# Four small edits to a scatter-add kernel: a PSUM bank, a split one-hot, a later payload and a later flag product

## The chip, the core and the metric

The kernel runs on one core of one Trainium2 chip. Its engines are TensorE (PE in the profile, its weight loads PEld), VectorE (DVE), ScalarE (ACT), GpSimd (POOL) and SyncE (SP), each with a queue of its own that it works off in order. The metric is the device time of one execution in microseconds, the median of several runs.

## The reference

There are 4096 nodes with 128 float features each and 65536 edges, drawn at random. Every edge adds the feature row of its source node to the output row of its destination node.

```python
def reference(node_features, edge_index_src, edge_index_dst):
    output = np.zeros((num_nodes, dim), dtype=np.float32)
    for i in range(len(edge_index_src)):
        output[edge_index_dst[i]] += node_features[edge_index_src[i]]
    return output
```

## The kernel before, in words

The kernel never gathers a row. It sorts the edges by blocks of 128 nodes in two passes, and then does the whole sum as dense matmuls: for every block of destinations and every block of sources, a product of two one-hot matrices gives the 128x128 matrix of edge counts between them, and that matrix is multiplied by the features of the sources.

**First pass.** The edges are split into 24 chunks, taken as six quads (`NQ = 6`, so index 4 is the fifth quad). For each quad, `buckets1` makes one-hots of the destination block, `counts` makes ranks out of them with matmuls into four PSUM banks that carry the tag `psA` (ScalarE copies each out as `cum`), and `move1` moves the edges: for each of four parts `l`, VectorE makes one-hots `p` of the ranks (line 210, the helper `onehot`, three windows each) and TensorE multiplies them with the payloads into the bank `psm` (line 295). Behind the four parts ScalarE copies `psm` out as `sbk` and `sa` (lines 299 and 300). `psm` has the tag `misc`, which is a single bank. While the moves of quad `q` run, the function `beside` does the bucket work of group 0 for earlier quads: `buckets0` compares `sbk` (VectorE, line 380), TensorE makes column sums of that (`pst`, line 389), `scan0` scans these on VectorE (line 394), `counts0` and `ranks0` go on with them.

**Second pass and main loop.** Eight groups of four destination blocks follow (`GROUPS`), each with four slots of the main loop, 32 slots in all. In a slot, `blocks` makes the count matrices of 8 steps in two halves of four (line 688, sixteen matmuls a half, into `psA` banks, copied out as `a` by ScalarE, line 690), and `product` multiplies them by the features (line 695, eight matmuls a half, into `pso`). The one-hots `oh` of a slot are made one slot ahead by `onehots`: one VectorE instruction for the source keys (`slo`) and one for the destination keys (`dlo`), over 32 columns each; only for slot 0 these are split into two parts of 16 columns. Beside this, the groups to come are prepared by the steps of `pass2(g)`: which step runs in which slot is written out in `STEPS` (group g from 3 on in slots 4g-10, 4g-9, 4g-8, 4g-4 and 4g-3). The first step of a group makes `buckets` (VectorE, line 538) and then, on GpSimd, `two_chunks`, the sums of two chunks (line 554); the second is `before_all`, twelve matmuls on those sums into `psb` (line 564, in the `misc` bank) and a ScalarE copy (line 566); the third is `running_by_two` (lines 577 and 581), `masked` (line 586) and `payloads` (line 547), all on GpSimd; the fourth adds halves and makes ranks; the fifth moves the edges. A dictionary `owed` holds back the payloads of group 3: they run at the end of the first step of group 4.

After every fourth slot `evacuate` and `finish` bring the sums of four slots out: ScalarE copies `pso`, TensorE transposes it into `psx` (line 314, the `misc` bank), ScalarE copies that to `rows` (line 316), and SyncE writes it out. At the end of slot 28 (`slots - 4`) `flag` checks whether any bucket overflowed: VectorE reduces the ranks to a column `fall`, TensorE sums it over the partitions into `psf` (line 712, `misc` too), and VectorE writes a flag (line 713) that decides about a general path behind the kernel.

The order of the work on each engine is the order of the program; nothing is rearranged. A tile waits for the readers of the tile that had its buffer before.

Of the kernel before, what the change touches and what calls it, by code (L numbers as in the profile page):

```python
# [8 lines left out]
P = 128  # L9
F32 = mybir.dt.float32  # L10
# [11 lines left out]
NQ = NCH // 4  # L22
# [18 lines left out]
def kernel(  # L41
# [32 lines left out]
    with ExitStack() as fast:  # L74
        fast.enter_context(tc.manual_schedule())
        _fast(fast, tc, node_features, src32, dst32, out, ident, fmax, flag_i, T)
# [6 lines left out]
def _fast(ctx, tc, X, src32, dst32, out, ident, fmax, flag_i, T):  # L83
# [7 lines left out]
    ps = ctx.enter_context(tc.tile_pool(name="ps", bufs=2, space=bass.MemoryType.PSUM))  # L91
# [115 lines left out]
    def onehot(dst, keys2, n, m=P, io=None, m0=0):  # L207

        io = (piota if io is None else io)[:, None, m0:m0 + m].to_broadcast([P, n, m])
        V.tensor_tensor(  # L210
            out=dst.rearrange("p i (m k) -> p i m k", k=2),
            in0=io.rearrange("p i (m k) -> p i m k", k=2),
            in1=keys2[:, :, None, :].to_broadcast([P, n, m // 2, 2]), op=OP.is_equal)
# [63 lines left out]
    def place(q):  # L277

        at = (q % 2 * QH + q // 2) * 4
        return slice(at, at + 4)  # L280
# [2 lines left out]
    sbk = sb1.tile([P, NCH, NB], BF16, name="sbk")  # L283

    def move1(q, meanwhile):
        psm = ps.tile([P, 512], F32, name="psm", tag="misc", bufs=1)
        for l in range(4):
            t = p1[l // 2]
            n = len([j for j in range(NJ) if j * NCH + q * 4 + l < T])
            for j0, j1, m0, m1 in WIN:  # L290
                j1 = min(j1, n)
                onehot(t[:, l % 2, j0:j1, m0:m1], rank1[q][:, l, j0:j1], j1 - j0, m1 - m0, m0=m0)
            meanwhile(l)
            for j in range(n):
                PE.matmul(out=psm[:, l * 64:(l + 1) * 64], lhsT=t[:, l % 2, j, :],  # L295
                          rhs=v1[q][:, 4 * j + l].bitcast(BF16),
                          start=j == 0, stop=j == n - 1)
        pv = psm[:, :256].rearrange("p (l b k) -> p l b k", l=4, k=2)
        S.copy(out=sbk[:, place(q), :], in_=pv[:, :, :, 0])
        S.copy(out=sa[:, place(q), :], in_=pv[:, :, :, 1])  # L300
# [4 lines left out]
    def evacuate(k, pso):  # L305
        res = sb2.tile([P, 512], F32, name="res")
        S.copy(out=res[:], in_=pso[:])
        done.append((k, res))

    def finish():  # L310
        for k, res in done:
            psx = ps.tile([P, 512], F32, name="psx", tag="misc", bufs=1)
            for i in range(4):
                PE.transpose(psx[:, i * P:(i + 1) * P], res[:, i * P:(i + 1) * P], ident[:])
            rows = sb2.tile([P, 4, P], F32, name="rows", bufs=1)
            S.copy(out=rows[:].rearrange("p i f -> p (i f)"), in_=psx[:])
            nc.sync.dma_start(
                out=out[4 * k * P:4 * (k + 1) * P, :].rearrange("(i p) f -> p i f", p=P),
                in_=rows[:])
        done.clear()  # L320
# [180 lines left out]
    for q in range(NQ):  # L501
        if q == NQ - 1:
            p2c = sb1.tile([P, 2, NCH, P], BF16, name="p2c", tag="o2")
            p2b += [p2c[:, 0], p2c[:, 1]]
        move1(q, during(q))
        if q + 4 < NQ:
            buckets1(q + 4)
            column_sums1(q + 4)
        if q < 2:
            x_part(q + 2, 0)  # L510
        if q + 2 < NQ:
            spread1(q + 2)
# [6 lines left out]
    def pass2(g):  # L519
# [143 lines left out]
        both = tuple(each(*fs) for fs in zip(*[p[:2] for p in pairs])) + pairs[1][2:]  # L663
        ahead = owed.pop(g - 1, lambda: None)
        fs = [running_by_two, masked]
        if g == 3:
            owed[g] = payloads
        else:
            fs.append(payloads)
# [4 lines left out]
    def onehots(slot):  # L674

        oh = sb1.tile([P, 2, 4 * 8, P], BF16, name="oh", tag=f"t2{slot % 2}")
        at = slot % 4 * 32
        for i, n in ((0, 16), (16, 16)) if slot == 0 else ((0, 32),):
            if i:
                buckets_2()  # L680
            for k, io in ((0, piotas), (1, piota)):
                onehot(oh[:, k, i:i + n], keys2[slot // 4][k][:, at + i:at + i + n], n, io=io)
        return oh

    def blocks(k, oh, a):
        psa = ps.tile([P, 512], F32, name="psa", tag="psA", bufs=4)
        for i in range(4):
            PE.matmul(out=psa[:, i * P:(i + 1) * P], lhsT=oh[:, 0, 4 * k + i, :],  # L688
                      rhs=oh[:, 1, 4 * k + i, :], start=True, stop=True)
        S.copy(out=a[:, k, :], in_=psa[:])  # L690

    def product(k, slot, a, pso):
        s = slot % 4 * 8 + k
        for v in range(2):
            PE.matmul(out=pso[:], lhsT=xr[s // 16][:, s % 16, v, :], rhs=a[:, k, :],  # L695
                      start=s == 0 and v == 0, stop=s == NB - 1 and v == 1)

    def flag():

        ng = len(GROUPS)  # L700
        full = sb1.tile([P, NCH * NB], BF16, name="full", tag="o0")
        V.tensor_single_scalar(out=full[:], in_=sbk[:].rearrange("p c b -> p (c b)"), scalar=0.5,
                               op=OP.is_gt)
        V.tensor_reduce(out=fmax[:, ng:ng + 1], in_=full[:], op=OP.add, axis=AX.X)
        V.tensor_reduce(out=fmax[:, :ng], op=OP.max, axis=AX.X,
                        in_=rank2[:].rearrange("p g j c u k -> p g (j c u) k")[..., 0])
        V.tensor_scalar(out=fmax[:, :ng], in0=fmax[:, :ng], scalar1=63.5, scalar2=float(2 * P * T),
                        op0=OP.is_gt, op1=OP.mult)
        fall = sb1.tile([P, 1], F32, name="fall")
        V.tensor_reduce(out=fall[:], in_=fmax[:, :ng + 1], op=OP.add, axis=AX.X)  # L710
        psf = ps.tile([P, 512], F32, name="psf", tag="misc", bufs=1)
        PE.matmul(out=psf[:1, :1], lhsT=fall[:], rhs=one[:], start=True, stop=True)
        V.tensor_single_scalar(out=flag_i[:], in_=psf[:1, :1], scalar=float(P * T),
                               op=OP.not_equal)

    todo = [[]] + [pass2(g) for g in range(1, len(GROUPS))]

    def run(fs):
        for f in fs:
            f()  # L720
# [36 lines left out]
    sums_1()  # L757
    counts_1()
    oh = onehots(0)
    slots = NB  # L760
    prev, pso = None, None
    late = {}
    for slot in range(slots):
        for f in late.pop(slot, ()):
            f()
        steps = [todo[g].pop(0) for g in STEPS.get(slot, ())]
        late[slot + 2] = [f for st in steps for f in st[2:]]
        cur = oh
        if slot + 1 < slots:
            oh = onehots(slot + 1)  # L770
        if slot == 0:
            halves_1()
        if slot - 1 not in LATER and slot != 1:
            run(st[0] for st in steps)
        a = sb1.tile([P, 8, 4 * P], F32R, name="a", tag=f"A{slot % 2}")
        if slot % 4 == 0:
            pso = ps.tile([P, 512], F32, name="pso", tag="pso", bufs=1)
        for k in range(4):
            blocks(k, cur, a)
        if slot == 0:  # L780
            for k in range(4):
                product(k, slot, a, pso)
            before_all_2()
            running_2()
        if slot == 1:
            ranks_1()
            run(st[0] for st in steps)
        if slot > 1:
            for k in range(4, 8):
                product(k, *prev)  # L790
            if prev[0] % 4 == 3:
                evacuate(prev[0] // 4, prev[2])
        for k in range(4, 8):
            blocks(k, cur, a)
        if slot - 1 in LATER:
            run(later)
            run(st[0] for st in steps)
        if slot == 2:
            payloads_2()
        for k in range(4, 8) if slot == 0 else range(4):  # L800
            product(k, slot, a, pso)
        finish()
        later = [st[1] for st in steps if len(st) > 1]
        if slot not in LATER:
            run(later)
        prev = (slot, a, pso)
        if slot == slots - 4:
            flag()
    assert not any(todo[1:])
    for k in range(4, 8):  # L810
        product(k, *prev)
# [90 lines left out]
```

## Time and profile before

| | |
|---|---|
| median of three runs | 279.84 us (279.72 to 279.94) |
| the profiled execution | 280.0 us, of which 278.3 us lie in the span of its instructions |
| busy: TensorE, its weight loads | 264.6 us (95%), 223.2 us (80%) |
| busy: VectorE, ScalarE, GpSimd | 240.9 us (87%), 188.8 us (68%), 197.2 us (71%) |
| mean granted TensorE clock | 0.998 of full speed |

The span is what the profile covers, from the first instruction to the last. Busy shares are averages over stages with different limits; a matmul's end is modelled, so the busy time of TensorE is a little too long and its idle time a little too short.

### The profile page before, as it was taken

Reading aid. Unit: us, or ns where it says so; the run is one execution under the profiler, and the core shown is the slowest. Engines: PE = TensorE matmul, PEld = TensorE weight load, DVE = VectorE, ACT = ScalarE, POOL = GpSimd, SP = SyncE. Lnnn points to the kernel's source line nnn. Section 1 sums busy time; section 2 is a strip of 40 time slices with the busy share of each in tenths; the row PEclk is TensorE's granted clock in tenths of the full one; section 3 lists DMA queues with packets and bytes.
Section 4 is the critical chain, followed back from the end, with each engine's and each line's share of the span. In section 5 each row is a group of like instructions: output and inputs, shape, how many; then the busy total and the mean of one; then the engine's idle time right before and its main releaser. Section 6 shows DMA issues by size and latency. Waiting matters only on the chain.

```text
span 278.3 us, 8026 instructions
## 1 busy us (share of the span) xinstructions
PE 264.6 (95%) x3466; PEld 223.2 (80%) x3466; DVE 240.9 (87%) x239; ACT 188.8 (68%) x403; POOL 197.2 (71%) x205
## 2 busy tenths in 40 slices
PE   7599998998999999999989999999999999999994
PEld 6488887895888788888878888888888788877882
DVE  3989986999999989999997999899898899887801
ACT  1867777247676757777657687867776776877771
POOL 7499999848699989999998997999699400000000
PEclk9999999999999999999999999999999999999999
DMA  7800000000000010001000100100010001001001
GB/s 231 224 2 4 5 5 2 2 5 0 2 2 1 2 38 2 2 1 40 2 0 0 40 2 1 40 4 0 2 38 2 0 2 38 2 2 39 0 4 39
DMA packets 8725, 5.77 MB, mean 21 GB/s; under 512 B 240, under 2 KB 8432, under 8 KB 8688
## 3 DMA queue, kind: packets, MB, share of 16 engines
q1 hardware_dynamic: 8272, 4.59, 5.8%
q10 hardware_dynamic: 416, 0.66, 0.8%
q8 instruction: 27, 0.44, 0.7%
q14 instruction: 10, 0.08, 0.1%
HBM read 3.15 MB, written 2.10 MB: 19 GB/s over the span
## 4 chain that ended last, share of the span: by engine, by line
PE 63%; POOL 16%; DVE 11%; ACT 4%; issue 3%; DMA 2%; DVEq 0%; POOLq 0%
PE pso L695 29%; PE psa L688 14%; DVE oh L210 7%; PE psm L295 5%; POOL cum L586 5%; POOL v L547 4%; PE psr L257 3%; POOL cum L577 3%; ACT cum L252 3%; POOL two L554 2%; POOL cum L581 2%; PE ps L615 2%; DMA raw<-in_edge_index_dst_dram 2%; PE psc L249 2%; PE psc L245 2%
## 5 line engine op out<-in xcount | busy, mean ns | idle before, releaser
L690 ACT CAST a<-psa 128x512 fp32r<-128x512 f32 x256 | 131.7, 604 | 27.1 <-PE psa L688 27.0
L695 PE MATMUL pso<-a,xr 128*128 128x512 f32 x512 | 133.6, 403 | 0.1
L695 PEld LDWEIGHTS pso<-a,xr 128*128 128x128 f32 x512 | 91.1, 189 | 17.5 <-ACT a L690 1.6
L210 DVE TENSOR_TENSOR oh<-psi,slo 128x4096 bf16<-128x4096 uint16 (+1 forms) x33 | 73.2, 2219 | 9.1 <-PE psa L688 9.1
L210 DVE TENSOR_TENSOR oh<-psi,dlo 128x4096 bf16<-128x4096 uint16 (+1 forms) x33 | 73.1, 2216 | 0.0
L688 PE MATMUL psa<-oh 128*128 128x128 bf16 x1024 | 68.6, 220 | 1.0 <-ACT cum L648 0.6
L688 PEld LDWEIGHTS <-oh 128*128 128x128 bf16 x1024 | 57.9, 98 | 13.4 <-issue 12.2
L547 POOL TENSOR_TENSOR v<-oh,sa 128x512 bf16<-128x512 bf16 x42 | 42.6, 1056 | 1.9 <-DVE oh L538 1.9
L586 POOL TENSOR_TENSOR cum<-cum,oh 128x512 bf16<-128x512 bf16 x36 | 40.6, 1169 | 0.0
L273 POOL TENSOR_TENSOR v<-oh,kab 128x704 f32<-128x704 bf16 x24 | 32.9, 1406 | 5.5 <-ACT kab L185 4.4
L210 DVE TENSOR_TENSOR p<-psi,rank 128x448 bf16<-128x448 uint16 (+3 forms) x72 | 29.7, 479 | 0.0
L577 POOL TENSOR_TENSOR cum<-cum,two 128x256 bf16<-128x256 bf16 x25 | 19.2, 769 | 6.9 <-ACT cum L566 5.3
L252 ACT ACTIVATE cum<-psc,minus 128x512 bf16<-128x512 f32 (+1 forms) x36 | 21.0, 650 | 2.4 <-PE psc L249 1.7
L295 PE MATMUL psm<-v,p 128*128 128x64 bf16 x512 | 18.5, 193 | 1.6 <-ACT sa L300 1.4
L295 PEld LDWEIGHTS <-p 128*128 128x128 bf16 x512 | 16.8, 98 | 2.0 <-issue 1.3
L554 POOL TENSOR_TENSOR two<-oh 128x512 bf16<-128x512 bf16 x15 | 17.1, 1170 | 0.0
L581 POOL TENSOR_TENSOR cum<-cum,oh 128x512 bf16<-128x512 bf16 x15 | 17.0, 1163 | 0.0
L210 DVE TENSOR_TENSOR p2a<-psi,rank 128x3072 bf16<-128x3072 uint16 (+2 forms) x14 | 14.4, 1063 | 1.6 <-ACT rank L603 1.6
L210 DVE TENSOR_TENSOR p2c<-psi,rank 128x3072 bf16<-128x3072 uint16 x8 | 13.6, 1746 | 0.0
L249 PEld LDWEIGHTS <-sums 128*128 128x128 bf16 x126 | 10.0, 98 | 4.5 <-DVE sums L236 0.9
L249 PE MATMUL psc<-identb,sums 128*128 128x128 bf16 x126 | 12.7, 219 | 0.6 <-DVE sums L236 0.6
L245 PE MATMUL psc<-oh,early 128*128 128x512 bf16 (+1 forms) x36 | 13.0, 362 | 0.0
(105 smaller groups left out, 240.9 us busy)
## 6 DMA issues: line engine op xcount, KB each, us to landing
xf<-in_node_features_dram SPq DMA_DIRECT2D x4, 512.0 KB, 7.4
out_dram<-rows SPq DMA_DIRECT2D x7, 256.0 KB, 2.3
raw<-in_edge_index_src_dram ACTq DMA_DIRECT2D x1, 512.0 KB, 4.7
raw<-in_edge_index_dst_dram SPq DMA_DIRECT2D x1, 512.0 KB, 5.0
out_dram<-rows SPq DMA_DIRECT2D x1, 128.0 KB, 1.9
out_dram<-rows ACTq DMA_DIRECT2D x1, 128.0 KB, 2.1
```

The costliest lines, as they stand in the source:

```text
L210: V.tensor_tensor(out=dst.rearrange("p i (m k) -> p i m k", k=2), in0=io.rearrange("p i (m k) -> p i m k", k=2), in1=keys2[:, :, None, :]. ...
L249: PE.matmul(out=psc[:, (j - j0) * P:(j - j0 + 1) * P], lhsT=sums[q][:, j - 1:j].to_broadcast([P, P]), rhs=identb[:], start=False, stop=j = ...
L252: S.activation(out=cum[:, :, 4 * j0:4 * (j0 + n)], func=RELU, bias=minus[:], in_=psc[:, :n * P].rearrange("p (t b) -> p b t", b=NB))
L273: G.tensor_tensor(out=v1[q][:, l::4], in0=oh1q(q)[:, l::4], op=OP.mult, in1=kab[:, q, l::4, None].to_broadcast([P, NJ, NB]))
L295: PE.matmul(out=psm[:, l * 64:(l + 1) * 64], lhsT=t[:, l % 2, j, :], rhs=v1[q][:, 4 * j + l].bitcast(BF16), start=j == 0, stop=j == n - 1)
L547: G.tensor_tensor(out=T2["v"][:, c:c + 4], in0=T2["o"][:, c:c + 4], op=OP.mult, in1=sa[:, c:c + 4, None, d0:d0 + 4].to_broadcast([P, 4, NB ...
L554: G.tensor_tensor(out=T2["t"][:, i:i + 4], in0=oh[:, i:i + 4, 0], in1=oh[:, i:i + 4, 1], op=OP.add)
L577: G.tensor_tensor(out=cum[:, :, 2 * i], in0=cum[:, :, 2 * i - 2], in1=two[:, :, i - 1], op=OP.add)
L586: G.tensor_tensor(out=flat("c")[:, c:c + 4], in0=flat("c")[:, c:c + 4], in1=flat("o")[:, c:c + 4], op=OP.mult)
L688: PE.matmul(out=psa[:, i * P:(i + 1) * P], lhsT=oh[:, 0, 4 * k + i, :], rhs=oh[:, 1, 4 * k + i, :], start=True, stop=True)
L690: S.copy(out=a[:, k, :], in_=psa[:])
L695: PE.matmul(out=pso[:], lhsT=xr[s // 16][:, s % 16, v, :], rhs=a[:, k, :], start=s == 0 and v == 0, stop=s == NB - 1 and v == 1)
```

## The change

Four edits. The moves of the fifth quad write into one of the four `psA` banks instead of the `misc` bank. The one-hots of slot 4 are made in two parts of 16 columns, as those of slot 0 are. The payloads of group 4 are held back as those of group 3 are, so that they run behind the sums of two of group 5. The flag's check is cut in two: VectorE's reductions stay at the end of slot 28, and the matmul and the final comparison move to the end of slot 30.

```diff
     def move1(q, meanwhile):
-        psm = ps.tile([P, 512], F32, name="psm", tag="misc", bufs=1)
+        tag, bufs = ("psA", 4) if q == NQ - 2 else ("misc", 1)
+        psm = ps.tile([P, 512], F32, name="psm", tag=tag, bufs=bufs)
...
         fs = [running_by_two, masked]
-        if g == 3:
+        if g in (3, 4):
             owed[g] = payloads
...
-        for i, n in ((0, 16), (16, 16)) if slot == 0 else ((0, 32),):
-            if i:
+        for i, n in ((0, 16), (16, 16)) if slot in (0, 4) else ((0, 32),):
+            if i and slot == 0:
                 buckets_2()
...
         V.tensor_reduce(out=fall[:], in_=fmax[:, :ng + 1], op=OP.add, axis=AX.X)
+        return fall
+
+    def flag_of_all(fall):
         psf = ps.tile([P, 512], F32, name="psf", tag="misc", bufs=1)
         PE.matmul(out=psf[:1, :1], lhsT=fall[:], rhs=one[:], start=True, stop=True)
...
         if slot == slots - 4:
-            flag()
+            fall = flag()
+        if slot == slots - 2:
+            flag_of_all(fall)
```

## Rows read from the trace of the kernel before

**Rows 1.** Waits between engines: who waited for whom; us in total, times, longest

```profile
ACT a L690 <- PE psa L688: 27.0, 39, 1.4
...
PE psm L295 <- ACT sa L300: 1.4, 2, 0.8
```

**Rows 2.** Stretches: length, then busy us (instructions) by engine, granted clock, DMA

```profile
47.54:57.15 9.61, 8.81 (x259) 8.51 (x260) 9.61 (x25) 2.78 (x13) 7.10 (x6) 1.00 0.02 3
92.60:253.00 160.40, 159.65 (x1684) 134.32 (x1685) 149.51 (x88) 116.59 (x248) 119.24 (x118) 1.00 0.04 11
146.99:170.74 23.75, 23.75 (x249) 19.99 (x246) 21.61 (x14) 17.98 (x39) 23.44 (x23) 1.00 0.04 12
```

**Rows 3.** Timeline, the moves: start, us, engine, instructions, [idle before, releaser]

```profile
47.77 0.77 PE L295 MATMUL psm<-v,p 128*128 128x64 bf16 x21 [0.82 <-ACT sa L300]
...
52.74 0.77 PE L295 MATMUL psm<-v,p 128*128 128x64 bf16 x21 [0.57 <-ACT sa L300]
...
56.73 0.42 DVE L380 TENSOR_TENSOR oh<-psi,sbk 128x512 bf16<-128x512 uint16 x1
...
57.34 0.24 PE L389 MATMUL pst<-ones,oh 128*128 128x1 bf16 x4
...
57.62 0.18 DVE L394 TENSOR_TENSOR_SCAN sums<-ones,pst 128x12 bf16<-128x12 bf16 x1 [0.47 <-PE pst L389]
```

**Rows 4.** Timeline, around the first blocks of slot 4

```profile
89.18 1.07 PE L688 MATMUL psa<-oh 128*128 128x128 bf16 x16
...
90.29 2.28 DVE L210 TENSOR_TENSOR oh<-psi,dlo 128x4096 bf16<-128x4096 uint16 x1
...
92.63 1.07 PE L688 MATMUL psa<-oh 128*128 128x128 bf16 x16 [0.48 <-DVE oh L210]
...
95.43 1.07 PE L688 MATMUL psa<-oh 128*128 128x128 bf16 x16
...
98.52 1.76 DVE L210 TENSOR_TENSOR p2a<-psi,rank 128x3072 bf16<-128x3072 uint16 x1 [1.55 <-ACT rank L603]
```

**Rows 5.** Timeline, the split one-hots of slot 0 and its first blocks

```profile
64.19 1.22 DVE L210 TENSOR_TENSOR oh<-psi,dlo 128x2048 bf16<-128x2048 uint16 x1
...
65.46 0.40 PE L688 MATMUL psa<-oh 128*128 128x128 bf16 x4
...
66.98 1.22 DVE L210 TENSOR_TENSOR oh<-psi,slo 128x2048 bf16<-128x2048 uint16 x1
```

**Rows 6.** Timeline, the preparation of group 5

```profile
135.77 1.75 DVE L538 TENSOR_TENSOR oh<-psi,sbk 128x3072 bf16<-128x3072 uint16 x1
...
136.56 6.08 POOL L547 TENSOR_TENSOR v<-oh,sa 128x512 bf16<-128x512 bf16 x6
...
142.60 3.40 POOL L554 TENSOR_TENSOR two<-oh 128x512 bf16<-128x512 bf16 x3
...
144.66 0.67 PE L564 MATMUL psb<-two,before 128*128 128x128 bf16 x8
...
146.05 0.38 PE L564 MATMUL psb<-two,before 128*128 128x128 bf16 x4 [0.73 <-POOL two L554]
...
146.99 4.27 POOL L577 TENSOR_TENSOR cum<-cum,two 128x256 bf16<-128x256 bf16 x5 [0.99 <-ACT cum L566]
```

**Rows 7.** Timeline, the same product in group 6

```profile
167.32 3.42 POOL L554 TENSOR_TENSOR two<-oh 128x512 bf16<-128x512 bf16 x3
...
171.26 0.84 PE L564 MATMUL psb<-two,before 128*128 128x128 bf16 x12
...
171.94 1.06 PE L688 MATMUL psa<-oh 128*128 128x128 bf16 x16
```

**Rows 8.** Timeline, the flag's product at the end of slot 28

```profile
253.19 0.60 PE L314 MATMUL psx<-ident,res 128*128 128x128 f32 x4
...
254.46 0.19 PE L712 MATMUL psf<-one,fall 128*1 128x1 f32 x2 [0.67 <-ACT rows L316]
...
254.58 1.07 PE L688 MATMUL psa<-oh 128*128 128x128 bf16 x16
```

## The prediction

> **What bounds the kernel now.** I read the waits between engines first, then the busy time by stretch, then the timeline around each place that the diff touches. In the waits view ScalarE waits 27.0 us for the block products, which means that it follows TensorE; TensorE itself is named in only a few lines, among them the moves' wait for the copies of the quad before [rows 1]. By stretch there are two regimes [rows 2]. From 47.54 to 57.15 us VectorE is busy 9.61 of 9.61 us and TensorE 8.81: here VectorE sets the pace. From 92.6 to 253.0 us TensorE is busy 159.65 of 160.40 us and VectorE 149.51: here TensorE sets the pace, and a gap in its row that goes away is time. The granted clock is 1.00 in both. So the question for each edit is whether its gap lies in the first regime or the second.
>
> One matter of reading goes ahead of the sums. A listed idle time of TensorE starts from the modelled end of the matmul before, which lies after the moment when the next could have started. I therefore count a gap from start to start, against the same sequence without a wait.
>
> **Fifth quad's moves in a bank of the counts.** In the profile TensorE's first matmul of the fifth quad waits 0.82 us, and that of the sixth 0.57 us, for the copy of the other quad's sums out of the one bank they share [rows 3]. With the fifth quad in the counts' four banks, its own first matmul waits for the fourth-last user of those banks, a count step whose copy stands ahead of the awaited one in ScalarE's queue, and the sixth finds its bank free since the fourth quad. Both waits go. But this is VectorE's stretch. TensorE, let in earlier, next stands at the bucket product of the fourth quad, behind VectorE's compare at 47.54, then at the next quad's bucket product behind the next such compare, then at the last one-hots of the sixth quad. VectorE's own list from 47.54 on has no hole to fill: its next wait comes at 57.62, for the bucket product that started at 57.34 [rows 3]. That product needs the compare that began at 56.73 and took 0.42, so ended at 57.15. TensorE got to it at 57.34 because of the work ahead of it in its queue; when that is earlier, it can start at about 57.21, taking 0.06 us from the end of a VectorE instruction to the matmul that it releases (90.29 + 2.28 to 92.63 in [rows 4]). Gain: 57.34 - 57.21 = **0.13 us**; bounds 0 and 0.19 (57.34 - 57.15). What hides the rest is VectorE's one-hots; without that cover the full 0.82 + 0.57 = 1.39 us would come out. The later users of the four banks each get another bank, but the order of copies in ScalarE's queue is the same and each bank still has three users between, so I cost the shift at nothing; if one was not free, a wait like the 0.57 would appear once.
>
> The Trainium skill's page Perfetto Trace Analysis, section Optimizing Tensor Performance, says that independent groups of matmuls should rotate through different banks, so that the copy out of one overlaps the next. The trace agrees that the copies stop TensorE, 0.82 and 0.57 us [rows 3]. By that rule alone the edit would be worth 1.39 us; by the full VectorE row it is worth 0.13.
>
> **Slot 4's one-hots in two parts.** Blocks start at 89.18, 92.63 and 95.43: 3.45 us where the next period takes 2.80. The loss is **0.65 us**, listed as 0.48, and its releaser is the one-hot that ran 90.29 to 92.57 over all 32 columns [rows 4]. In two parts, the first four blocks need only the first half. That a block waits for its half alone shows in slot 0, which is split already: its blocks began at 65.46, right after the half of 64.19 + 1.22, while the second half began only at 66.98 [rows 5]. In slot 4 the first of the two one-hots, of the same length, stood just ahead of 90.29, so the first halves would be done at about 90.29 - 2.28 + 2 x 1.22 = 90.45, and TensorE comes at 89.18 + 2.80 = 91.98, so nothing is left of the wait. The price is on VectorE: four instructions of 1.22 for two of 2.28, at most 0.32 us. It falls into the 1.55 us that VectorE waits at 98.52 for the ranks [rows 4], so it costs nothing; without that cover it is 0.32. Since that wait at 98.52 ends with a TensorE product and a ScalarE copy, VectorE's whole list behind it moves earlier by the same 0.65. Bounds of the gain: 0.48 and 0.65.
>
> **Group 4's payloads behind group 5's sums of two.** GpSimd runs group 4's payloads from 136.56 to 142.60 and then group 5's sums of two, which end at 146.00; the product that needs them starts at 144.66 with eight of its twelve matmuls and goes on at 146.05. In group 6 all twelve take 171.26 to 171.94, 0.057 us each, so the ninth was due at 144.66 + 8 x 0.057 = 145.12 [rows 6, 7]. The loss is 0.93 us (0.73 as listed). Behind the edit the sums start when their one-hots are there, 135.77 + 1.75 = 137.52, less the 0.78 us by which the two edits above bring VectorE forward, plus 0.1 of latency: 136.84, and end at 140.24, long before the product. The payloads run behind them to 136.84 + 3.40 + 6.04 = 146.28, and their own readers, the moves of group 4 in slot 13, come two slots, four periods of 2.80, behind the product in slot 11. What is queued behind the payloads on GpSimd are the running sums of group 5, which began at 146.99 [rows 6]; they now begin at 146.28, 0.71 earlier, while TensorE is 0.13 + 0.65 + 0.93 = 1.71 earlier. GpSimd has so lost 1.00 us against TensorE, and it has no hole to make it good: it is busy for 23.44 of the 23.75 us up to the end of group 6's sums of two at 170.74 [rows 2]. The last four of group 6's twelve products needed them at 171.26 + 8 x 0.057 = 171.71 [rows 7]: a reserve of 0.97, less 0.05 of latency. So about 0.1 us of wait appears there, and this edit brings 0.93 - 0.10 = **0.83 us**. Bounds: 0.93 if GpSimd comes as early as TensorE, and about 0 if it comes a whole microsecond later than I have it.
>
> **Flag's product two slots later.** At 254.46 the product of the flag waits 0.67 us for ScalarE's copy of the output rows out of the bank that both use, and the next blocks start 0.12 us later [rows 8]. The transposes ahead of it, at 253.19, end in the model at 253.79. Counted as in slot 4, where a listed 0.48 was 0.65 from start to start, the loss is 0.67 + 0.17 = **0.84 us**, bounds 0.67 and 0.84. At the end of slot 30 nobody has used that bank since the copy and the sum that it reads, ready here, is then 11 us old (four periods of 2.80), so it costs the same 0.12 there as here. VectorE's last step, the comparison, then sits behind the one-hots of slot 31, with all of slot 31's products still to come; the last transposes use its bank, a slot later.
>
> **The sum.** 0.13 + 0.65 + 0.83 + 0.84 = 2.45 us. The profiled execution took 280.0 us with a span of 278.3; it becomes 277.55, with a span near 275.9. Its time stands 0.16 above the median of the three runs, 279.84, so the median becomes **277.4 us**. By listed waits alone (0.48 + 0.73 + 0.67, and nothing from the moves) it would be 278.0.
>
> **The rivals.**
> 1. *The moves bring their whole wait.* If the one-hots were not the limit, the first edit gives 1.39 in place of 0.13: 277.4 - 1.26 = 276.1 us. For it: the two waits are real [rows 3]. Against it: 9.61 of 9.61 us on VectorE [rows 2]. Chance 0.06. It is the case that the rule of the Trainium skill's page Perfetto Trace Analysis, above, leads to.
> 2. *The wait moves on to group 6.* If VectorE's list does not come forward with slot 4, group 5's sums start 0.65 later than I have them, and the product of group 6 waits about 0.75 in place of 0.10: 278.1 us. For it: GpSimd is back to back from one group's sums to the next, and the reserve is just 0.97. Against it: VectorE's wait at 98.52 is for TensorE's own work. Chance 0.15.
> 3. *One part does not do what it says:* the blocks wait for the whole tile after all, or the flag's product meets another wait. That loses 0.65 or 0.84: 278.0 to 278.3 us. Against it: slot 0's halves [rows 5]. Chance 0.09.
> 4. *Slower.* One mechanism could do it: GpSimd falls so far behind in group 5, because the payloads now stand between the sums of two and the running sums, that TensorE stops at group 6's product for more than the change brings. To lose 2.45 us and another 0.6, the sums of two there would have to end some 3 us later than I have them, three instructions of GpSimd. At 3.5 us it gives 280.9. Against it: the payloads take 6.04 us before, beside the same one-hots of VectorE. Chance 0.04.
> 5. *No change:* the gaps return elsewhere in full, 279.8 us. VectorE's 149.51 of 160.40 us would have to be nearer to its limit than it is. Chance 0.06.
>
> **How the numbers follow.** The forecast, 277.0 to 278.0 us, has 0.60. The range reaches down to 276.9, which holds the upper bounds of the terms, and leaves out rival 1; it reaches up to 278.4, which takes in rivals 2 and 3 and the listed waits. It leaves out 0.16. Measured runs spread by about 0.1 us; I take 0.2%, 0.56 us, as what can be told from no change. Faster: 0.60 + 0.06 + 0.15 + 0.09, of which I take off 0.02 for mishaps together: 0.88. Same: 0.07. Slower: 0.05.
>
> **What the next profile would show.** Right: no wait of the moves for the copy of the quad before, yet the stretch up to the bucket product at 57.34 shorter by only 0.1 to 0.2 us; blocks of slot 4 at a period of 2.8; the twelve products of group 5 in 0.68 us, with a small wait, about 0.1, in group 6; the blocks behind the transposes of slot 28 some 0.44 us after them. Wrong: VectorE idle between 48 and 57 us, which would mean that TensorE led there; a wait for the sums of two in group 6 of 0.5 us or more; or a new line in TensorE's waits that names a bank of the counts.

## The result, and the profile after

The changed kernel takes 277.94 us (277.60 to 278.24, six runs), the kernel before, run beside it, 279.89 us (279.72 to 280.02). The ratio is 0.9918 with a 95% interval of 0.9903 to 0.9932. It was forecast faster, 277.4 us in a range of 276.9 to 278.4. The profiled execution, 277.6 us, was the fastest of the six; its span went from 278.3 to 275.9 us. In the other five the mean granted clock was lower, 0.991 to 0.994 beside 0.997. Only the profiled execution left rows that show where a clock falls; but in all fourteen kept traces of this document a mean below 0.995 goes with a fall in the first 15 us, ahead of everything that the change touches, and one of 0.996 or more goes without it. I take the five for such executions. They occur in both kernels and cost some 0.5 us; experiments 10 and 11 are about them.

In the lines shown here, line numbers behind the first edit are one to four higher than before. The page's first lines:

```profile
span 275.9 us, 8028 instructions
## 1 busy us (share of the span) xinstructions
PE 264.7 (96%) x3466; PEld 223.3 (81%) x3466; DVE 241.3 (87%) x241; ACT 188.7 (68%) x403; POOL 197.2 (71%) x205
```

TensorE does the same work (264.6 us before) in 2.4 us less span. The two instructions more are the split one-hots. The stretches that answer to [rows 2], from the same instructions to the same (length, then busy time by engine: PE, PEld, DVE, ACT, POOL; granted clock; DMA):

```profile
47.54:57.00 9.46, 8.66 (x242) 8.11 (x241) 9.45 (x25) 3.19 (x13) 7.10 (x6) 1.00 0.02 3
91.68:251.30 159.62, 159.61 (x1685) 134.21 (x1685) 150.75 (x90) 116.58 (x248) 119.82 (x119) 1.00 0.04 11
```

In the first, VectorE is still busy without a hole, 9.45 of 9.46 us: it still sets the pace. In the second, TensorE has 0.01 us of listed idle time left, where it had 0.75; the modelled ends of its matmuls hide the wait of 0.17 us that is left in group 6, below.

The timeline of the moves after, which answers to [rows 3] (start, us, engine, instructions, idle time before and its releaser):

```profile
46.18 1.39 PE L296 MATMUL psm<-v,p 128*128 128x64 bf16 x42
...
48.02 0.25 PE L390 MATMUL pst<-ones,oh 128*128 128x1 bf16 x4 [0.45 <-DVE oh L381]
...
51.05 1.39 PE L296 MATMUL psm<-v,p 128*128 128x64 bf16 x42
...
54.27 0.25 PE L390 MATMUL pst<-ones,oh 128*128 128x1 bf16 x4 [0.28 <-DVE oh L381]
...
56.58 0.41 DVE L381 TENSOR_TENSOR oh<-psi,sbk 128x512 bf16<-128x512 uint16 x1
...
57.05 0.25 PE L390 MATMUL pst<-ones,oh 128*128 128x1 bf16 x4
...
57.34 0.18 DVE L395 TENSOR_TENSOR_SCAN sums<-ones,pst 128x12 bf16<-128x12 bf16 x1 [0.35 <-PE pst L390]
```

The fourth quad's last matmuls and the fifth's first now stand in one row of 42, and so do the fifth's and the sixth's: both waits for the copy are gone. In their place TensorE waits 0.45 and 0.28 us for the bucket one-hots of VectorE. The bucket product of the sixth quad starts at 57.05 in place of 57.34. No new wait of TensorE for a bank of the counts is listed.

Slot 4, which answers to [rows 4]:

```profile
88.90 1.07 PE L689 MATMUL psa<-oh 128*128 128x128 bf16 x16
...
91.20 1.22 DVE L210 TENSOR_TENSOR oh<-psi,dlo 128x2048 bf16<-128x2048 uint16 x1
...
91.71 1.07 PE L689 MATMUL psa<-oh 128*128 128x128 bf16 x16
...
94.51 1.07 PE L689 MATMUL psa<-oh 128*128 128x128 bf16 x16
...
97.60 1.76 DVE L210 TENSOR_TENSOR p2a<-psi,rank 128x3072 bf16<-128x3072 uint16 x1 [0.79 <-ACT rank L604]
```

The blocks start 2.81 us after those before, where it was 3.45, while the last half of the one-hots is still running (91.20 to 92.42). VectorE's wait behind it, 0.79 us, is shorter than 1.55 but still there: the two instructions more found their cover.

Groups 5 and 6, which answer to [rows 6] and [rows 7]:

```profile
136.79 3.41 POOL L555 TENSOR_TENSOR two<-oh 128x512 bf16<-128x512 bf16 x3 [1.06 <-DVE oh L539]
...
140.15 6.09 POOL L548 TENSOR_TENSOR v<-oh,sa 128x512 bf16<-128x512 bf16 x6
...
143.74 0.84 PE L565 MATMUL psb<-two,before 128*128 128x128 bf16 x12
...
144.42 1.06 PE L689 MATMUL psa<-oh 128*128 128x128 bf16 x16
...
146.19 4.29 POOL L578 TENSOR_TENSOR cum<-cum,two 128x256 bf16<-128x256 bf16 x5
...
166.54 3.41 POOL L555 TENSOR_TENSOR two<-oh 128x512 bf16<-128x512 bf16 x3
...
169.38 1.01 PE L565 MATMUL psb<-two,before 128*128 128x128 bf16 x12
...
170.23 1.06 PE L689 MATMUL psa<-oh 128*128 128x128 bf16 x16
```

Group 5's twelve matmuls now run in one row, 0.68 us to the blocks behind them. Group 6's take 0.85 (169.38 to 170.23), 0.17 more than before: the sums of two end there at 169.95, while the ninth matmul was due at 169.38 + 8 x 0.057 = 169.84. That is GpSimd's lag. It is not the same in every execution: in the second trace of the changed kernel (experiment 10) the twelve take 0.99 us to the blocks behind them (169.38 to 170.37), so 0.31 more than before. The running sums start at 146.19, 0.80 earlier than before, while TensorE is by then (its blocks at 144.42 in place of 146.27) 1.85 earlier.

The end of slot 28 and of slot 30, which answer to [rows 8]:

```profile
251.48 0.60 PE L315 MATMUL psx<-ident,res 128*128 128x128 f32 x4
251.91 1.06 PE L689 MATMUL psa<-oh 128*128 128x128 bf16 x16
...
260.34 1.07 PE L689 MATMUL psa<-oh 128*128 128x128 bf16 x16
...
263.23 0.19 PE L716 MATMUL psf<-one,fall 128*1 128x1 f32 x2
263.36 1.07 PE L689 MATMUL psa<-oh 128*128 128x128 bf16 x16
```

The blocks of slot 29 follow the transposes by 0.43 us in place of 1.39. The flag's product costs 0.22 us in its new place: the period from 260.34 to 263.36 is 3.02 us where others are 2.80.

### The profile page after: what moved, and what is told of

Its sections match the earlier page's. It is cut to its first block, busy times and chain, and to the rows that moved or that the text cites. A ratio compares the mean times of both kernels' runs of the same rounds, so it can differ in the third digit from the quotient of the medians.

```text
span 275.9 us, 8028 instructions
## 1 busy us (share of the span) xinstructions
PE 264.7 (96%) x3466; PEld 223.3 (81%) x3466; DVE 241.3 (87%) x241; ACT 188.7 (68%) x403; POOL 197.2 (71%) x205
## 4 chain that ended last, share of the span: by engine, by line
PE 86%; ACT 5%; DVE 5%; DMA 2%; issue 1%; DVEq 0%; ACTq 0%
PE pso L696 44%; PE psa L689 20%; PE ps L616 4%; PE psm L296 3%; ACT cum L252 3%; PE psr L257 2%; PE psr L600 2%; DVE p L210 2%; DMA raw<-in_edge_index_dst_dram 2%; PE psb L565 2%; PE psc L249 2%; PE psc L245 2%; ACT cum L649 1%; PE psx L315 1%; DVE oh L210 1%
## 5 line engine op out<-in xcount | busy, mean ns | idle before, releaser
L210 DVE TENSOR_TENSOR p2c<-psi,rank 128x3072 bf16<-128x3072 uint16 x8 | 13.6, 1746 | 0.0
```

The lines of the kernel that those rows point to most:

```text
L210: V.tensor_tensor(out=dst.rearrange("p i (m k) -> p i m k", k=2), in0=io.rearrange("p i (m k) -> p i m k", k=2), in1=keys2[:, :, None, :]. ...
```

## The experiments

All kernels were run in rounds beside the kernel before, those down to both orders on one chip, the last four on another. Since the fall of the clock at the start adds some 0.5 us to an execution, the table gives, beside the median of all runs, the median of those whose mean granted clock was 0.996 or more ("at a full clock"); these I compare. The ratios and their intervals are of all runs.

| kernel | median of all (runs) | median at a full clock (runs) | before at a full clock (runs) | ratio, 95% interval |
|---|---|---|---|---|
| moves alone | 279.82 (12) | 279.73 (7) | 279.94 (16) | 0.9989, 0.9973 to 1.0006 |
| payloads alone | 279.69 (12) | 279.30 (5) | 279.94 (16) | 0.9975, 0.9961 to 0.9988 |
| split alone | 279.80 (12) | 279.37 (5) | 279.94 (16) | 0.9984, 0.9970 to 0.9997 |
| flag alone | 279.32 (12) | 279.20 (8) | 279.94 (16) | 0.9965, 0.9953 to 0.9976 |
| all four again | 278.09 (6) | 277.47 (1) | 279.99 (6) | 0.9921, 0.9904 to 0.9938 |
| all payloads behind | 277.42 (6) | 277.39 (4) | 279.99 (6) | 0.9903, 0.9885 to 0.9921 |
| buckets between | 277.37 (6) | 277.30 (5) | 279.99 (6) | 0.9898, 0.9881 to 0.9915 |
| both orders | 277.23 (6) | 277.09 (2) | 279.99 (6) | 0.9893, 0.9875 to 0.9911 |
| before, buckets between | 280.03 (11) | 280.02 (8) | 280.00 (5) | 0.9992, 0.9983 to 1.0001 |
| flag in another bank | 277.42 (4) | 277.41 (3) | 280.00 (5) | 0.9905, 0.9890 to 0.9920 |
| longer warm-up | 277.59 (4) | 277.59 (4) | 280.00 (5) | 0.9902, 0.9887 to 0.9918 |
| both orders, longer warm-up | 277.12 (4) | 277.12 (4) | 280.00 (5) | 0.9887, 0.9872 to 0.9902 |

**1. The first edit alone.**

```diff
-        psm = ps.tile([P, 512], F32, name="psm", tag="misc", bufs=1)
+        tag, bufs = ("psA", 4) if q == NQ - 2 else ("misc", 1)
+        psm = ps.tile([P, 512], F32, name="psm", tag=tag, bufs=bufs)
```

> The kernel before with only the first edit: the fifth quad's moves write into a bank of the counts. Theory (VectorE sets the pace between 47.5 and 57.2 us, so both waits of TensorE go but only the start of the sixth quad's bucket product moves, by some 0.1 to 0.3 us): 279.6 us, ratio 0.999, VectorE busy without a hole from 47.5 to 57 us. Rival (the two waits of 0.82 and 0.57 us come out in full): 278.4 us, ratio 0.995.

At a full clock 279.73 us beside 279.94: 0.2 us, and not the 1.4 of the waits that it removes. The ratio's interval alone would not tell 0.2 us from nothing, but the runs at a full clock hardly overlap (279.52 to 279.82 beside 279.78 to 280.12), and the trace shows where it comes from. The fourth quad's bucket compare before (the sixth quad's bucket product starts at 57.34 there [rows 3]):

```profile
47.54 0.42 DVE L380 TENSOR_TENSOR oh<-psi,sbk 128x512 bf16<-128x512 uint16 x1 [2.32 <-ACT sbk L299]
```

The same compare and product with this edit alone:

```profile
48.24 0.42 DVE L381 TENSOR_TENSOR oh<-psi,sbk 128x512 bf16<-128x512 uint16 x1 [2.33 <-ACT sbk L300]
...
57.76 0.25 PE L390 MATMUL pst<-ones,oh 128*128 128x1 bf16 x4
```

From the one to the other it is 9.80 us before and 9.52 here, 0.28 less (the whole profile is late by the fall of the clock at its start). The theory holds.

**2. The payloads alone.**

```diff
-        if g == 3:
+        if g in (3, 4):
             owed[g] = payloads
```

> The kernel before with only group 4's payloads behind group 5's sums of two. Theory (the gap of 0.93 us in front of group 5's last products goes, and GpSimd, whose list does not come forward with it, takes back 0.1 to 0.2 us at group 6's product): 279.1 us, ratio 0.997, a wait of TensorE for the sums of two in group 6 only. Rival (the wait moves on to group 6 in full): 279.8 us, ratio 1.000, a wait of some 0.7 us there.

At a full clock 279.30: 0.64 us. Group 5's wait is gone, and in group 6 the twelve matmuls take 1.00 us with the modelled end where they took 0.84:

```profile
170.93 1.00 PE L564 MATMUL psb<-two,before 128*128 128x128 bf16 x12
...
171.77 1.06 PE L688 MATMUL psa<-oh 128*128 128x128 bf16 x16
```

So 0.16 us of the 0.93 is taken back there, much as in the kernel with all four edits; the wait does not move on in full. That leaves 0.77 us, some 0.1 more than the run times show; the five runs at a full clock lie between 279.08 and 279.34.

**3. The split alone.**

```diff
-        for i, n in ((0, 16), (16, 16)) if slot == 0 else ((0, 32),):
-            if i:
+        for i, n in ((0, 16), (16, 16)) if slot in (0, 4) else ((0, 32),):
+            if i and slot == 0:
                 buckets_2()
```

> The kernel before with only slot 4's one-hots in two parts. Theory (TensorE no longer waits 0.65 us at slot 4; VectorE's list comes forward with it, but GpSimd's only by some 0.5 us, so group 5's product, still behind the payloads, waits a little longer than before): 279.3 us, ratio 0.998, the wait in group 5 up from 0.73 to about 0.9 us. Rival (it is taken back in full at that product): 279.8 us, ratio 1.000.

At a full clock 279.37: 0.57 us. The listed wait in group 5 is again 0.73 us, which I had expected to grow. But counted from start to start it did grow: the first eight matmuls start 0.60 us earlier than in [rows 6], the last four only 0.47:

```profile
144.06 0.79 PE L564 MATMUL psb<-two,before 128*128 128x128 bf16 x8
...
145.58 0.38 PE L564 MATMUL psb<-two,before 128*128 128x128 bf16 x4 [0.73 <-POOL two L554]
```

The modelled end of the eight matmuls hides the difference (0.79 us here, 0.67 in [rows 6]).

**4. The flag alone.**

```diff
         if slot == slots - 4:
-            flag()
+            fall = flag()
+        if slot == slots - 2:
+            flag_of_all(fall)
```

> The kernel before with only the flag's product two slots later. Theory (the wait for the bank goes, 0.84 us from start to start, and the product itself costs 0.1 to 0.2 us where it now stands): 279.1 us, ratio 0.997. Rival (the blocks behind the transposes meet another wait, for ScalarE's copies): 279.6 us, ratio 0.999.

At a full clock 279.20: 0.74 us, as theory had it. The four single gains sum to 0.21 + 0.64 + 0.57 + 0.74 = 2.16 us; together they gave 2.3 to 2.5 (279.9 or 280.0 to 277.6 or 277.5). Of the difference, 0.13 is what the split alone loses at group 5's product, where with all four edits nothing waits.

**5. All payloads behind the next group's sums.** The changed kernel, and:

```diff
-        if g in (3, 4):
+        if 3 <= g < len(GROUPS) - 1:
             owed[g] = payloads
```

> The changed kernel with the payloads of groups 5 and 6 held back as well, so that the sums of two of groups 6 and 7 run ahead of them. Theory (the 0.17 us by which the product of group 6 is now late is GpSimd's lag from group 5): the wait in group 6 goes, 0.17 us below the changed kernel, and no other appears. Rival (the late payloads of groups 5 and 6 hold up something else): no gain, or a wait of TensorE for the payloads in slots 17 or 21.

The wait in group 6 is gone, its twelve matmuls are back at their 0.84 us, and no other wait for GpSimd came up:

```profile
162.46 3.41 POOL L555 TENSOR_TENSOR two<-oh 128x512 bf16<-128x512 bf16 x3 [1.69 <-DVE oh L539]
...
169.50 0.84 PE L565 MATMUL psb<-two,before 128*128 128x128 bf16 x12
```

At a full clock 277.39 us beside 277.47 and 277.60 of the changed kernel: 0.1 to 0.2, of the size of the 0.17 us (0.31 in the changed kernel's second trace), though with so few runs the time alone would not show it.

**6. Bucket one-hots between.** The changed kernel, with another order on VectorE:

```diff
-    for cs in EARLY0:
-        permute0(0, cs)
+    permute0(0, EARLY0[0])
     buckets0(NQ - 1)
+    permute0(0, EARLY0[1])
```

> The changed kernel with the sixth quad's bucket one-hots put between the two early one-hots of group 0 on VectorE, in place of behind both. Theory (VectorE's order is what hides the rest of the first edit's gain): the bucket product starts some 0.3 us earlier and VectorE's hole before its scan closes, 0.2 to 0.3 us below the changed kernel. Rival (TensorE's own list sets that point): no gain.

```profile
55.89 0.27 ACT L300 CAST sbk<-psm 128x128 bf16<-128x128 f32 x1 [1.94 <-PE psm L296]
...
56.19 0.42 DVE L381 TENSOR_TENSOR oh<-psi,sbk 128x512 bf16<-128x512 uint16 x1
...
56.80 0.24 PE L390 MATMUL pst<-ones,oh 128*128 128x1 bf16 x4
...
57.13 0.17 DVE L395 TENSOR_TENSOR_SCAN sums<-ones,pst 128x12 bf16<-128x12 bf16 x1
```

The bucket one-hots start at 56.19, right behind ScalarE's copy, where they stood behind a second one-hot until 56.58; the bucket product comes 0.25 us earlier and VectorE's hole of 0.35 us before the scan is closed. At a full clock 277.30 us: some 0.2 to 0.3 below the changed kernel. So VectorE's order held 0.25 us of the first edit's gain. It does not account for the rest: of the two waits' 1.39 us, 0.29 and 0.25 have come out, and no run here brings out the other 0.85. Group 6's product still waits for GpSimd in this kernel: it takes 0.95 us to the blocks behind it (169.16 to 170.11), 0.27 more than without a wait.

**7. The same order in the kernel before.** The same diff, without any edit of the change.

> The kernel before (no edit of the change) with the sixth quad's bucket one-hots between the two early one-hots of group 0 on VectorE. Theory (with the shared bank TensorE ends the sixth quad's moves too late for this order to help; it needs the first edit): no gain over the kernel before, 0 to 0.15 us slower, ratio 1.000. Rival (the order is worth its 0.25 us by itself): 279.85 us beside 280.1, ratio 0.999.

At a full clock 280.02 beside 280.00: nothing. VectorE now waits for the copy, which the shared bank makes late:

```profile
56.88 0.27 ACT L299 CAST sbk<-psm 128x128 bf16<-128x128 f32 x1 [1.44 <-PE psm L295]
...
57.18 0.42 DVE L380 TENSOR_TENSOR oh<-psi,sbk 128x512 bf16<-128x512 uint16 x1 [0.59 <-ACT sbk L299]
...
58.12 0.17 DVE L394 TENSOR_TENSOR_SCAN sums<-ones,pst 128x12 bf16<-128x12 bf16 x1
```

(All times of this profile are some 0.45 us late from the fall of the clock at its start.) So the order needs the bank: 0.2 us for the bank alone, nothing for the order alone, some 0.4 to 0.5 for both (the order's 0.2 to 0.3 was measured with the other three edits in place).

**8. Both orders** (5 and 6 together).

> The changed kernel with both of the last two edits. Theory: they lie in different stretches and add, 0.4 us below the changed kernel. Rival: TensorE, early by another 0.25 us, finds GpSimd late at group 5's product and loses it there.

At a full clock 277.09 us in two runs, 0.4 to 0.5 below the changed kernel: they add. Nothing is lost at GpSimd: group 5's and group 6's products both take 0.68 us to the blocks behind them (143.98 to 144.66, 169.62 to 170.30).

**9. The flag's product in another bank.** The changed kernel, with the product back in slot 28:

```diff
-        psf = ps.tile([P, 512], F32, name="psf", tag="misc", bufs=1)
+        psf = ps.tile([P, 512], F32, name="psf", tag="ps2", bufs=1)
...
         if slot == slots - 4:
-            fall = flag()
-        if slot == slots - 2:
-            flag_of_all(fall)
+            flag_of_all(flag())
```

> The changed kernel with the flag's product back in slot 28, but in another bank (that of the permuted quads, free there). Theory (what held it was the bank and not its place): within 0.15 us of the changed kernel. Rival (the place in slot 28 costs by itself, since ScalarE's copy of the rows or VectorE's sum comes too late there): 0.5 to 0.8 us above the changed kernel.

```profile
251.55 0.60 PE L315 MATMUL psx<-ident,res 128*128 128x128 f32 x4
252.08 0.19 PE L716 MATMUL psf<-one,fall 128*1 128x1 f32 x2
...
252.20 1.07 PE L689 MATMUL psa<-oh 128*128 128x128 bf16 x16
```

The product follows the transposes by 0.53 us and the blocks by 0.65, without a wait; in the changed kernel the same work took 0.43 + 0.22. At a full clock 277.41 us, no slower. What held it was the bank, not the place.

**10. The changed kernel again, and the clock at the start.**

> The changed kernel once more, to see how far its runs at a full granted clock in the first 20 us differ from those in which the clock falls there. Theory (the fall lies ahead of everything that the change touches and comes and goes in both kernels): runs at a full clock near 277.6 us, those with the fall some 0.4 to 0.6 us above, the kernel before likewise, ratio 0.992. Rival (the change itself makes the clock fall more often): most runs of the changed kernel at a mean clock below 0.995, most of before above it.

One run of six at a full clock, 277.47 us, the other five 277.68 to 278.22. In the two measurements of the changed kernel 10 of 12 executions had the fall; of the kernel before 23 of 45 on that chip, and 10 of 15 on another. Taken alone, 10 of 12 looks like more. But the other versions that hold all four edits and the same 60 warming matmuls (all payloads behind, buckets between, both orders, flag in another bank) had it in 8 of 22, so with the edits it is 18 of 34 and in the kernel before 33 of 60. So these runs do not show that the change makes the fall more frequent, and the fall is over before the first edited instruction runs. In the four traces that show it, the blocks around 89 us come 0.5 to 0.7 us later than in traces without it.

**11. Longer warm-up.** The changed kernel, and then the version with both orders, each with 72 in place of 60 warming matmuls:

```diff
-WARM = 60
+WARM = 72
```

> The changed kernel with 72 in place of 60 warming matmuls ahead of the first column sums, which shortens TensorE's idle stretch there. Theory (the clock falls after about 9.6 us in some executions because of the idle stretch ahead of it): no or few runs with a mean clock below 0.996, median near 277.6 us. Rival (whether it falls is set by when the clock rose, not by the stretch): as many runs with the fall as in the changed kernel, median 277.9 to 278.1 us.

> The version with both orders and with 72 warming matmuls. Theory: 277.1 us in all runs. Rival: the fall in half of the runs, median 277.3 us.

None of the eight runs has the fall, where 77 of the 153 of all kernels with 60 warming matmuls had it. The stretch from 9.6 to 13.6 us, first of an execution with it (of experiment 7; its second line is the middle of the stretch alone), then with the longer warm-up (columns as above; the first busy time is TensorE's, the granted clock is the third number from the end):

```profile
9.60:13.60 4.00, 3.91 (x32) 2.91 (x33) 3.88 (x8) 3.79 (x7) 2.86 (x3) 0.57 0.81 201
...
10.40:13.40 3.00, 3.00 (x21) 2.11 (x19) 3.00 (x3) 2.79 (x6) 2.66 (x2) 0.50 0.77 190
```

```profile
9.60:13.60 4.00, 3.02 (x48) 2.38 (x49) 4.00 (x10) 4.00 (x8) 2.70 (x2) 1.00 0.81 202
```

The 0.57 is a mean: between 10.4 and 13.4 us the clock is at 0.50, the lower of TensorE's two levels (1.2 of 2.4 GHz), and in the whole stretch TensorE gets through 32 matmuls where it otherwise does 48. In the two executions the warm-up and the first column sums behind it ran so:

```profile
1.32 6.09 PE L127 MATMUL psw<-ones 128*128 128x128 bf16 x60 [1.32 <-POOL ones L122]
8.15 0.70 PE L227 MATMUL pst<-ones,oh 128*128 128x1 bf16 x22 [0.74 <-DVE oh L210]
```

```profile
1.32 6.97 PE L127 MATMUL psw<-ones 128*128 128x128 bf16 x72 [1.32 <-POOL ones L122]
8.31 0.70 PE L227 MATMUL pst<-ones,oh 128*128 128x1 bf16 x22
```

With 72 the idle 0.74 us is filled here, and in the other trace with 72 it is 0.22. But the length of the idle stretch, which the theory named, does not decide. In the four traces with the fall (moves alone, payloads alone, both orders, and this one) it was 0.74 to 1.05 us; in the eight others with 60 matmuls it was 0.48 to 0.52 in three, and 1.52 to 2.02 in five, none of which has a fall. What goes with it is how long the 60 matmuls themselves took: 5.80 to 6.09 us in the four, 6.33 to 6.36 and 4.82 to 5.33 in the others. At the 0.057 us of such a matmul later on, 60 would take 3.4 us, so a part of them, and not always the same part, ran slower, although the granted clock of the profile reads 1.00 there. That bears out the rival, by which it matters when in the warm-up the clock rose, and not the theory. With so few traces it is argued and not shown, and why 72 matmuls keep the clock up stays open.

With both orders and the longer warm-up the kernel takes 277.12 us (277.07 to 277.20), ratio 0.9887 (0.9872 to 0.9902), the lowest median over all runs of any version; without the longer warm-up the same kernel has 277.09 at a full clock.

## Why the prediction was right

**The forecast.** The span was to be near 275.9 us and is 275.9; the profiled execution 277.55 and is 277.6. The median came out 0.5 us above its forecast for a reason that no term held: five of six executions had the clock's fall at the start. The profile of before showed a granted clock of 1.00 there, and a single profile could not show that it is not always so. The range held it only by its upper side, which had been set for rivals 2 and 3 and the listed waits, not for this: that part is luck.

**The moves** were put at 0.13 us with 0.19 as the upper bound, and with 1.39 as a rival. The traces give 0.29, the run alone 0.2. The mechanism stands: both waits gone, two new ones for VectorE, so the rival is out. The term itself came as put: the bucket product started 0.19 us behind the end of its compare (57.15 to 57.34) and now starts 0.06 behind it (56.99 to 57.05). What was missing is that VectorE's list, which I took as fixed, came forward by 0.15 (56.73 to 56.58). Its busy share of 9.61 of 9.61 us had hidden two small waits, since a listed instruction of VectorE ends some 0.08 us after the next has started (47.54 + 0.42 = 47.96, the next at 47.88). The twelve one-hots in front of the second-last bucket compare, and ScalarE's copy ahead of the last one, before, then the one-hots after:

```profile
49.13 4.84 DVE L210 TENSOR_TENSOR p<-psi,rank 128x448 bf16<-128x448 uint16 x12
...
56.44 0.27 ACT L299 CAST sbk<-psm 128x128 bf16<-128x128 f32 x1 [1.44 <-PE psm L295]
```

```profile
49.12 4.76 DVE L210 TENSOR_TENSOR p<-psi,rank 128x448 bf16<-128x448 uint16 x12
```

The one-hots take 0.08 less; the profile names no releaser, and I take it for a wait for a buffer that TensorE still read. And the last compare started at 56.73 only when ScalarE's copy was there (56.44 + 0.27 = 56.71). The rule of the Trainium skill's page Perfetto Trace Analysis (section Optimizing Tensor Performance), that groups rotate through banks, was right about the wait and would have been wrong about the time by 1.1 us. With VectorE's order changed as well (experiments 6 and 7) the bank is worth 0.4 to 0.5 us.

**The split** was put at 0.65 and is 0.64 in the trace (3.45 to 2.81), 0.57 alone, where group 5's product takes back 0.13. Its cost on VectorE was hidden by the wait that was named.

**The payloads** were put at 0.83, from 0.93 less 0.10 at group 6; the trace gives 0.93 less 0.17, its second execution 0.93 less 0.31. The lag was there because the mechanism was: the sums of two had to wait for their one-hots (1.06 us of idle time on GpSimd), and the payloads then stood ahead of the running sums. Experiment 5 shows it from the other side. Rivals 2 and 4, the wait that moves on or grows, were this same mechanism with another size. Rivals 3 and 5 did not come either: each edit alone gave its gain.

**The flag** was put at 0.84 and is 1.39 - 0.43 - 0.22 = 0.74: the product costs 0.22 in its new place and not 0.12. The step that was a little off is the price of the product between two rows of other matmuls, which the wait in the row of before had hidden. Set against 0.43 and 0.22 us, the listed wait of 0.67 was short of the gap by 0.07 us only; the 0.17 had been carried over from slot 4.

The sum of the traces is 0.29 + 0.64 + 0.76 + 0.74 = 2.43 us, beside the forecast's 2.45 and 2.4 of the span. The mechanisms were right; that the sum is met to 0.02 us is luck, since the moves brought 0.16 more and the payloads and the flag 0.07 and 0.10 less than their terms.

## What to carry to other kernels

A wait that the profile lists is worth what it says only where its engine leads the stretch; look at the busy time of each engine in just that stretch first. A busy share of 100% still left 0.15 us of small waits on VectorE here. Count a TensorE gap from start to start against the same sequence without a wait, since the listed idle time was 0.17, 0.20 and 0.07 us too short in the gaps of slot 4, of group 5 and of the flag. And when a piece of work is pushed back on a queue, add up by how much everything behind it comes late against the engine that it feeds: the next group's reserve, here 0.97 us, is what it may cost for nothing.

## What the runs showed that I had not expected

In about half of the executions with 60 warming matmuls the mean granted clock was low, and the four of them that left a trace show the clock at 0.57 or 0.58 in the mean between 9.6 and 13.6 us, behind the warming matmuls. It cost about 0.5 us; with twelve warming matmuls more it stayed up in 8 of 8 runs. A product of one column in fp32, 0.19 us long, cost 0.22 us of TensorE's time between two rows of other matmuls.
